# Output weight's fourth tile staged in the other weight pool, and eight woven products moved ahead of the first carry's key norm

## The chip, the cores and the metric

The kernel runs on one core of one Trainium2 chip. Such a core has a matrix engine (PE, with a weight-load path that the profile calls PEld), a vector engine (DVE), an activation engine (ACT), a general engine (POOL) and a queue engine (SP) that issues most transfers. All work on a common on-chip memory, and PE's results land in PSUM banks from which DVE and ACT read them. The metric is the device time of one execution in microseconds (us); less is better.

## The reference

One layer of a network is applied to 128 context tokens and 512 latent tokens of width 1024 (640 columns together). The layer has two branches, a recurrence over time with eight heads of 64 in two directions and an attention; their outputs are gated, summed and multiplied by the output weight `w_out`, and a feed-forward block follows:

```python
merged = (jax.nn.sigmoid(gate_rw) * (o_rw @ p["w_o_rwkv"])
          + jax.nn.sigmoid(gate_na) * (o_na @ p["w_o_na"]))
x = x + g1 * (merged @ p["w_out"])
h2 = _rmsnorm(x, p["norm2_g"]) * (1.0 + sc2) + sh2
x = x + g2 * ((jax.nn.silu(h2 @ p["ffn_w1"]) * (h2 @ p["ffn_w3"])) @ p["ffn_w2"])
```

In the recurrence the keys are normalised per head (the "key norm"): `kk = kk * lax.rsqrt(jnp.sum(kk * kk, axis=-1, keepdims=True) + L2_EPS)`. Everything is float32.

## The kernel before, in words

**Products.** A float32 factor is split into a high part `hi` and a rest `lo`, and a product is made of three matmuls, hi·hi, hi·lo and lo·hi. A weight tile of 128 x 1024 is loaded by SP into a staging buffer `wst` (`wdma`, line 166), and `wcast` (line 187) makes `whi` and `wlo` from it. On one path ACT makes `whi` (line 194) and DVE the rest (line 197). On the other path (`eng is pool`) ACT first writes the negative high part into `wlo` (line 192), POOL then issues a transfer that adds `wst` onto it (line 193), and ACT makes `whi` as well. A tile's products can start once its `whi` is there, and those with `wlo` once the transfer has landed.

**Weight pools.** `weights(stack, n, m)` opens a pool with n staging buffers and m pairs of `whi` and `wlo`; the buffers of a pool are used in turn, so a new tile waits until the tile that had the buffer is through. The first pool (index 0) has two of each and lives to the end. A second pool with two of each is opened at line 1731 for the first half of the output weight, and closed again at line 1738; at line 1761 a third pool with one staging buffer and two pairs takes its place, and its memory, like that of the residual `x2` and the gate rows `G` (lines 1741 and 1750), lies where the second pool and its neighbours were. From line 1762 on `rot` holds pool 0 and the third pool, and `wdma` takes them alternately.

**Output weight.** `w_out` has eight tiles: 0 to 3 give the first 512 output columns, 4 to 7 the other 512. `tok_gen` (line 289) goes through a list of tiles: for each it calls `wload` and yields one matmul at a time over five token blocks (30 per tile). Tile 0 (`c0`) is loaded at line 1700 into pool 0, tiles 1, 2 and 3 into the second pool; with two buffers there, tile 3 takes those of tile 1. Tile 4 is the next to use pool 0, where it follows the last merge tile (`b3`); tile 5 goes to the third pool, 6 to pool 0 after `c0`, 7 to the third. The matmuls of tile 0 are partly interleaved with the last merge (`last_gen`). Between the halves DVE adds the gated first half to the residual (`add_gated`, lines 1757 and 1758), which reads `G` and `x2` and frees the PSUM banks that the second half then takes. The feed-forward's first two tiles (`W` in the table `n2`) follow in the same staging buffers.

**The weave.** In the recurrence stage (four groups `ct` of two heads, each with `main`, `inv`, `carry`, `out`) the small matmuls of a dependent chain are interleaved with big independent ones, "products", drawn from the stream `fill` (line 803): projections, gates and merges of 48 or 36 matmuls each. The table `PRM["plan"]` says for each step of each stage how many products go ahead (first number), and then by how much of the side work goes on (line 1617). In the carry the side work is the preparation of the next group, `prep` (line 1635): ACT squares the keys (line 662), five column blocks of two matmuls each sum them (line 666), then the low-rank projections follow (lines 647 and 649), and later a transposition (line 681). `beside` (line 522) draws on it within a budget and runs due deferred steps first. All products left over are drawn by `need` at line 1701.

**Order.** In these stages the order of PE (and inside most blocks also of ACT, DVE and POOL) is that of the program. SP's order is not: the framework's scheduler places its transfers by its own timeline. SP works strictly in its order, so a transfer that waits for its buffer holds up those behind it. In the block of lines 1733 to 1737 only PE and DVE are in program order, so the scheduler places ACT's and POOL's casts there too.

Of the kernel before, what the change touches and what calls it, by code (L numbers as in the profile page):

```python
# [27 lines left out]
    order=("l0 l1 k0 r0 v0 l2 g0 g1 g2 k1 g3 r1 g4 g5 v1 g6 g7 k2 r2 g8 g9 v2 g10 g11 k3 r3 g12 g13 v3 g15 g14 a0 a1 a2 "  # L28
     "a3 b0 b1 b2 b3"),
# [2 lines left out]
        ("0.0.0 2.0.0 2.0.1 4.0.0 2.0.1 2.0.1 4.0.1 4.0.1 4.0.1 2.0.0 4.0.0 2.0.0 2.0.0 10.0.0 2.0.0 "  # L32
         "2.0.0 2.0.0 10.0.0 2.0.0 2.0.0 2.0.0 2.0.0 2.0.0 2.0.0 2.0.0 2.0.0 2.0.0 2.0.0 2.0.0 2.0.0 "
         "5.0.0 24.0.0 20.0.0 10.0.0 8.0.0 8.0.0 0.0.0"),
        ("10.0 1.0 7.1 5.2 0.0 7.1 7.2 0.0 7.1 7.2 0.0 8.1 12.2 0.0 7.1 7.2 0.0 7.1 7.2 0.0 6.1 6.2 "
         "0.0 8.1 7.2 6.0"),
        "22.0 2.0 2.0 2.0",
        ("6.0.0 0.0.0 2.0.1 4.0.0 1.0.0 2.1.1 2.1.1 2.1.1 2.1.1 1.1.1 10.0.0 3.1.0 2.0.0 2.0.0 2.0.0 "
# [72 lines left out]
def V(ap, dims, off=0):  # L111

    return bass.AP(ap.tensor, ap.offset + off, [list(ap.ap[0])] + [list(d) for d in dims])
# [3 lines left out]
def body(ctx: ExitStack, tc: tile.TileContext, xs, xp, cols, consts, w_ada, b_row, w_rw, w_qkv,  # L117
# [3 lines left out]
    pe, act, dve, pool, sp = nc.tensor, nc.scalar, nc.vector, nc.gpsimd, nc.sync  # L121
# [13 lines left out]
    wpool, rot = [], []  # L135
# [8 lines left out]
    def nm(s):  # L144
        cn[0] += 1
        return f"{s}_{cn[0]}"
# [16 lines left out]
        return K[64 * h:64 * h + 64, KO["ident"] + 64 * h:KO["ident"] + 64 * h + 64]  # L163


    def wdma(src, home=None):
        if len(rot) > 1 and home is None:
            rot.append(rot.pop(0))
        pl, nst, nhl = (rot if home is None else wpool)[-1 if home is None else home] if rot else wpool[-1]
        st = pl.tile([P, 1024], F32, tag="wst", bufs=nst, name=nm("wst"))  # L170
        n = src.shape[1]
        if len(src.shape) == 3:
            sp.dma_start(V(st[:, :], [[src.shape[2], n], [1, src.shape[2]]]), src)
            n *= src.shape[2]
        else:
            sp.dma_start(st[:, :n], src)
        return st, n, pl, nhl

    pend, off, hold, gtag = [], [0], [False], ["fl"]
# [1 line left out]
    def later(fn, cost=(0.5, 0), more=0):  # L181
        if off[0]:
            pend.append([off[0] + more, cost, fn])
        else:
            fn()

    def wcast(w, eng=None):
        st, n, pl, nhl = w
        hi = pl.tile([P, 1024], F32R, tag="whi", bufs=nhl, name=nm("whi"))
        lo = pl.tile([P, 1024], F32R, tag="wlo", bufs=nhl, name=nm("wlo"))  # L190
        if eng is pool:
            act.activation(lo[:, :n], st[:, :n], AF.Copy, scale=-1.0)  # L192
            pool.dma_start(lo[:, :n].bitcast(F32), st[:, :n], accum_op=ALU.add)  # L193
        act.copy(hi[:, :n], st[:, :n])  # L194
        if eng is not pool:
            def low(a, b):
                dve.tensor_tensor(out=lo[:, a:b], in0=st[:, a:b], in1=hi[:, a:b].bitcast(F32), op=ALU.subtract)  # L197

            if len(gtag) > 1:
                low(0, 512)  # L200
                later(lambda: low(512, n), (0, 0), -off[0] + 5)
            else:
                low(0, n)
        return hi, lo

    def wload(src, eng=None):
        return wcast(wdma(src), eng)
# [22 lines left out]
    def drain(g):  # L230
        for _ in g:
            pass
# [56 lines left out]
    def tok_gen(pss, pp, lhs_hl, chunks, kts, toks, tag="acc", bufs=5, tail=1, keep=None, eng=None, late=()):  # L289


        pss.update((i, pp.tile([P, 512], F32, tag="tp" if i == 5 else tag, bufs=3 if i == 5 else bufs,
                               name=nm("acc"))) for i in toks)
        lhs = lhs_hl if callable(lhs_hl) else lambda p_, kt, ts_: lhs_hl[p_][:, kt, ts_]
        last = len(kts) - 1
        ws, n0 = [] if keep is None else keep, len(chunks) - tail
        for ci, src in enumerate(chunks):
            ws.append(src if isinstance(src, (tuple, list)) else wload(src, eng))
            ks = [2 * ci + k for k in range(2)]

            if ci >= n0:
                order = [(ki, i) for i in toks for ki in range(2 * n0, last + 1)] if ci == len(chunks) - 1 else ()
            else:
                order = [(ki, i) for tk in (toks[:4], toks[4:]) for ki in ks for i in tk]
            ns = ((0, 1), (2,)) if ci in late else ((0, 1, 2),)
            for n, ki, i in ((n, *p_) for g in ns for p_ in order for n in g):
                kt = kts[ki]
                hi, lo = ws[ki // 2]
                ts_ = slice(min(i, 4) * 128, min(i, 4) * 128 + 128)
                a, b = (256 * (i - 4), 256 * (i - 3)) if i > 3 and 5 in toks else (0, 512)  # L310
                cs_ = slice(ki % 2 * 512 + a, ki % 2 * 512 + b)
                for x, w in (((0, hi), (1, hi), (0, lo))[n],):
                    pe.matmul(pss[i][:, a:b], lhs(x, kt, ts_), w[:, cs_], start=ki == 0 and n == 0,  # L313
                              stop=ki == last and n == 2)
                    yield
# [124 lines left out]
    def blkch(b):  # L440
        return [w_qkv[b * 4 + q] for q in range(4)]
# [80 lines left out]
    def beside(gen, budget):  # L522

        a = d = 0
        while a < budget[0] and d < budget[1]:
            if pend and pend[0][0] <= 0:
                _, c, fn = pend.pop(0)
                fn()
            else:
                c = next(gen, None)  # L530
                if c is None:
                    return
            a, d = a + c[0], d + c[1]
# [308 lines left out]
    with s1:  # L842
# [25 lines left out]
        with s1a:  # L868
            for b, dst, gcol in ((0, qT, dcol(dqg)), (1, kT, col("kg"))):
                pss = tok_block(pp, (hh, hl), blkch(b), list(range(8)), range(5)) if b else psq  # L870
# [9 lines left out]
                for i in range(5):  # L880
# [21 lines left out]
                    for f in range(4):  # L902
                        src = pst[:, f * 128:(f + 1) * 128]
                        if i < 4:
                            out = V(dst[f], [[1, 2], [8, 64]], 2 * i)
                            src = V(src, [[64, 2], [1, 64]])
# [8 lines left out]
            pss = tok_block(pp, (hh, hl), blkch(2), list(range(8)), range(5))  # L915
# [20 lines left out]
        with ExitStack() as s1b:  # L936
# [128 lines left out]
            with tc.manual_schedule(engines=FIRST):  # L1065
                for k, step in enumerate(PRM["na"].split()):
                    a, p, b, q, n, s_ = (int(x) for x in (step + ".0").split(".")[:6])
# [31 lines left out]
    with ExitStack() as s3:  # L1099
# [542 lines left out]
        with tc.manual_schedule(engines=FIRST):  # L1642
# [4 lines left out]
            for ct in range(4):  # L1647
# [8 lines left out]
                late = [lambda: st_load(0, 0, act), lambda: st_load(0, 1, act)] if ct == 0 else []  # L1656
# [43 lines left out]
            c0 = wload(w_out[0], pool)  # L1700
# [25 lines left out]
    def w_out_gen(pss, ws, toks, **kw):  # L1726
        return tok_gen(pss, pp, (mh, ml), ws, list(range(8)), toks, **kw)

    pss = {}
    trp = open_pool(hs, "trp")  # L1730
    weights(hs, 2, 2)
    w0 = w_out_gen(pss, [c0] + [w_out[q] for q in range(1, 4)], range(5), eng=pool, late=(0, 1, 2))
    with tc.manual_schedule(engines=MANUAL | {mybir.EngineType.DVE}):
        for h, _ in enumerate(last_gen()):
            for _ in range(PRM["lw"][h]):
                next(w0)
        drain(w0)
    hs.close()
    nstack.close()
    xpool = open_pool(ctx, "xpool")  # L1740
# [127 lines left out]

    with tc.manual_schedule(engines=FIRST):
        w1s = []  # L1870
        beside(w_out_gen(pss, [wload(w_out[4], pool)] + [w_out[4 + q] for q in range(1, 4)], (0, 1, 2), tail=2, keep=w1s))
        beside(w_out_gen(pss, w1s, (3, 4), tail=2))
    hstack.close()

# [363 lines left out]
    with tc.manual_schedule(engines=FIRST):  # L2238
# [8 lines left out]
        for part, fs in enumerate(fts):  # L2247
# [3 lines left out]
            for j, ft in enumerate(todo):  # L2251
# [13 lines left out]
                n = len(todo)  # L2265
# [18 lines left out]
            for n in range(2):  # L2284
                pss = {}
# [117 lines left out]
```

## Time and profile before

| | us |
|---|---|
| time, median of 3 runs | 1138.34 |
| lowest and highest run | 1136.46, 1139.86 |
| the profiled execution's own time | 1138.35 |
| its span, first to last instruction | 1136.2 |
| PE busy in the span | 1100.7 |
| DVE, ACT, POOL busy | 811.7, 571.5, 244.4 |
| mean granted PE clock | 0.995 |

A view of the timeline gives the start of a row of like instructions in us from the span's start, their time together, engine, line, operation, output and inputs, their count, and in brackets how long the engine stood idle just before and which engine's work ended that. The view of waits sums such idle times by who waited for whom: us in total, times, longest. The view of stretches gives, for each stretch of time, its length, busy us and instruction count of each engine, then the granted PE clock (1.00 is full speed), the busy share of the transfer engines and their rate. A row "SPq" is a transfer's place in SP's queue; its time spans from the first to the last issue of the row, waits between them included.

### The profile page before, as it was taken

How to read it: one execution, taken by the hardware profiler on the slowest of the kernel's cores; microseconds unless marked ns; L12 is line 12 of the kernel's file. 1: busy time of each engine (PE TensorE's matmuls, PEld its weight loads, DVE VectorE, ACT ScalarE, POOL GpSimd, SP SyncE). 2: the span in 40 equal slices, each digit the busy share in tenths (PEclk: the TensorE clock that was granted, in tenths of full speed). 3: DMA queues.
4: the chain of work that ended last, by engine and by line, in shares of the span. 5: the costliest groups of instructions: out<-in, count | busy, mean ns of one | idle time of the engine just before them, and what ended most of it. 6: DMA issues, size and time to landing. Idle time of an engine off the chain costs nothing. (4 is left out here: it accounts for less than half of the span.)

```text
span 1136.2 us, 27125 instructions
## 1 busy us (share of the span) xinstructions
PE 1100.7 (97%) x11118; PEld 973.2 (86%) x11118; DVE 811.7 (71%) x1709; ACT 571.5 (50%) x1106; POOL 244.4 (22%) x318
## 2 busy tenths in 40 slices
PE   6999999999999999999999989999999999999998
PEld 4688878799888988888898768998999989989987
DVE  4565465769558947945787826899788888889854
ACT  4444566664565565567443424564453543444430
POOL 1163244320101112110100421151212112131100
PEclk9999999999899999999999999999999999999999
DMA  9862687654423443343734773476567567675622
GB/s 342 271 116 87 203 276 241 200 153 130 105 65 92 115 128 94 93 124 93 267 107 129 237 220 114 146 184 173 144 170 183 144 162 177 164 176 140 159 86 93
DMA packets 72995, 179.05 MB, mean 158 GB/s; under 512 B 8708, under 2 KB 23684, under 8 KB 72872
## 3 DMA queue, kind: packets, MB, share of 16 engines
q1 hardware_dynamic: 58488, 140.86, 37.8%
q0 software_dynamic: 12368, 33.56, 16.2%
q10 hardware_dynamic: 2016, 2.90, 0.8%
q8 instruction: 87, 1.43, 0.5%
q14 instruction: 36, 0.29, 0.1%
HBM read 137.81 MB, written 16.94 MB: 136 GB/s over the span
## 5 line engine op out<-in xcount | busy, mean ns | idle before, releaser
L1932 PE MATMUL f<-t,whi 128*128 128x320 f32 x640 | 141.8, 309 | 1.1 <-ACT whi L1977 0.8
L1932 PE MATMUL f<-b,whi 128*128 128x320 f32 x608 | 135.0, 310 | 0.4 <-DVE b L214 0.4
L225 PE MATMUL fl<-h,whi 128*128 128x320 f32 x672 | 122.5, 321 | 0.7 <-ACT U L542 0.7
L1932 PEld LDWEIGHTS f<-t,whi 128*128 128x128 f32 x640 | 106.9, 188 | 1.9 <-ACT whi L1977 1.3
L225 PEld LDWEIGHTS fl<-h,whi 128*128 128x128 f32 x672 | 101.2, 188 | 6.1 <-ACT U L542 0.9
L1932 PEld LDWEIGHTS f<-b,whi 128*128 128x128 f32 x608 | 101.8, 188 | 1.2 <-issue 0.6
L1932 PE MATMUL f<-t,wlo 128*128 128x320 f32 x320 | 99.0, 309 | 0.2 <-DVE wlo L1980 0.2
L1932 PE MATMUL f<-b,wlo 128*128 128x320 f32 x304 | 94.0, 309 | 0.1
L194 ACT CAST whi<-wst 128x1024 fp32r<-128x1024 f32 (+1 forms) x67 | 69.0, 1031 | 49.5 <-PE acc L313 34.3
L313 PE MATMUL acc<-whi,h 128*128 128x512 f32 x240 | 77.8, 398 | 1.3 <-DVE h L438 1.1
L1977 ACT CAST whi<-ws 128x1024 fp32r<-128x1024 f32 x40 | 42.1, 1052 | 68.6 <-PE f L1932 40.1
L197 DVE TENSOR_TENSOR wlo<-wst,whi 128x1024 fp32r<-128x1024 f32 (+2 forms) x47 | 48.0, 1032 | 26.2 <-ACT whi L194 25.5
L193 POOL DMA_DIRECT2D wlo<-wst x28 | 24.9, 890 | 186.8 <-ACT wlo L192 171.1
L225 PE MATMUL fl<-h,wlo 128*128 128x320 f32 x336 | 62.3, 317 | 0.0
L1932 PEld LDWEIGHTS f<-t,wlo 128*128 128x128 f32 x320 | 60.1, 188 | 0.5 <-DVE wlo L1980 0.5
L1932 PEld LDWEIGHTS f<-b,wlo 128*128 128x128 f32 x304 | 57.1, 188 | 0.4 <-DVE wlo L1980 0.4
L1991 POOL TENSOR_TENSOR ws<-wst 128x512 f32<-128x512 f32 x20 | 30.6, 1530 | 122.2 <-DVE wlo L1980 81.7
L1980 DVE TENSOR_TENSOR wlo<-ws,whi 128x1024 fp32r<-128x1024 f32 x40 | 53.6, 1340 | 4.1 <-ACT whi L1977 4.1
L1475 DVE TENSOR_TENSOR ZV<-w,Dt 64x128 f32<-64x128 f32 x64 | 18.5, 289 | 53.1 <-PE w L1463 51.9
L313 PEld LDWEIGHTS acc<-whi,h 128*128 128x128 f32 x240 | 44.6, 188 | 13.3 <-issue 2.0
L225 PEld LDWEIGHTS fl<-h,wlo 128*128 128x128 f32 x336 | 51.2, 188 | 1.8
L984 POOL TENSOR_TENSOR L<-L,m 128x384 f32<-128x384 f32 (+1 forms) x40 | 32.1, 824 | 92.5 <-DVE m L983 68.6
(381 smaller groups left out, 2827.2 us busy)
## 6 DMA issues: line engine op xcount, KB each, us to landing
wst<-in_w_dram SPq DMA_DIRECT2D x58, 512.0 KB
wst<-in_w_rw_dram SPq DMA_DIRECT2D x31, 512.0 KB
wlo<-wst POOLq DMA_DIRECT2D x28, 512.0 KB, 4.5
wa<-in_w_ada_dram SPq DMA_DIRECT2D x22, 512.0 KB
f<-in_w_ada_dram SPq DMA_DIRECT2D x18, 512.0 KB
t<-in_w_dram SPq DMA_DIRECT2D x16, 512.0 KB
wst<-in_w_qkv_dram SPq DMA_DIRECT2D x12, 512.0 KB
o<-o_d SPq DMA_DIRECT2D x14, 320.0 KB
```

The lines of the kernel that those rows point to most:

```text
L193: pool.dma_start(lo[:, :n].bitcast(F32), st[:, :n], accum_op=ALU.add)
L194: act.copy(hi[:, :n], st[:, :n])
L197: dve.tensor_tensor(out=lo[:, a:b], in0=st[:, a:b], in1=hi[:, a:b].bitcast(F32), op=ALU.subtract)
L225: pe.matmul(ps[:, :t1 - t0], w[:, a:a + 128], x[:, k0 + kt, t0:t1], start=n == 0, stop=n == 3 * nk - 1)
L313: pe.matmul(pss[i][:, a:b], lhs(x, kt, ts_), w[:, cs_], start=ki == 0 and n == 0, stop=ki == last and n == 2)
L984: pool.tensor_tensor(out=L, in0=L, in1=V(m[:, :], [[0, w]], 3), op=ALU.mult)
L1475: dve.tensor_tensor(out=V(ZV[own, l + 1, h, :], [[128 * dl, 2], [1, 64]]), in0=V(pn[own, :], [[64, 2], [1, 64]], 64 * g), in1=V(Dt[own, 0, ...
L1932: pe.matmul(ps[:, :H2], w_[:, c_], x_[:, kt, :], start=first and kt + n == 0, stop=last and kt == 3 and n == 2, skip_group_check=more)
L1977: act.copy(r[0][:, :width], src())
L1980: dve.tensor_tensor(out=r[1][:, :width], in0=src(), in1=r[0][:, :width].bitcast(F32), op=ALU.subtract)
L1991: eng_x(PRM["se"][i - 1]).tensor_tensor(out=o_, in0=x, in1=y, op=op)
```

## The change

Three edits:

1. In the plan of the first carry (`ct` = 0) the fourth entry, at the end of the first step, is 13.2 where it was 5.2: thirteen products instead of five are drawn there before the side work with the key norm's matmuls goes on. All other entries stay, so each later point of the plan has drawn eight products more, until the last `need` draws eight fewer.
2. Tile 3 of the output weight is handed to `tok_gen` as a function, called when its turn comes, which loads it into pool 0 (`wdma(w_out[3], 0)`) and casts it on the POOL path as before. In pool 0 it takes the buffers of `b3`; tile 4 then takes those of `c0`, tile 6 those of tile 3, and the feed-forward's first tile those of tile 4. `wdma` gets its pool from `wpool[home]` also while `rot` is empty.
3. Loads made by `wdma` with a plain source after tile 4, within the second half's first block (tiles 5, 6, 7 and the feed-forward's first two), get an order without a wait: they stand behind tile 3's load in SP's queue.

```diff
-        ("10.0 1.0 7.1 5.2 0.0 7.1 7.2 0.0 7.1 7.2 0.0 8.1 12.2 0.0 7.1 7.2 0.0 7.1 7.2 0.0 6.1 6.2 "
+        ("10.0 1.0 7.1 13.2 0.0 7.1 7.2 0.0 7.1 7.2 0.0 8.1 12.2 0.0 7.1 7.2 0.0 7.1 7.2 0.0 6.1 6.2 "
...
+    sent, behind = [], [None]
+
     def wdma(src, home=None):
         if len(rot) > 1 and home is None:
             rot.append(rot.pop(0))
-        pl, nst, nhl = (rot if home is None else wpool)[-1 if home is None else home] if rot else wpool[-1]
+        pl, nst, nhl = wpool[home] if home is not None else (rot or wpool)[-1]
...
-            sp.dma_start(st[:, :n], src)
+            sent.append(sp.dma_start(st[:, :n], src))
+            if behind[0]:
+                tc.add_manual_dep(sent[-1].ins, behind[0].ins.name, mybir.DependencyInfo(
+                    mybir.DependencyClass.NoSync, mybir.DependencyReason.DATA), reason="order")
...
-            ws.append(src if isinstance(src, (tuple, list)) else wload(src, eng))
+            ws.append(src if isinstance(src, (tuple, list)) else src() if callable(src) else wload(src, eng))
...
-    w0 = w_out_gen(pss, [c0] + [w_out[q] for q in range(1, 4)], range(5), eng=pool, late=(0, 1, 2))
+    w0 = w_out_gen(pss, [c0, w_out[1], w_out[2], lambda: wcast(wdma(w_out[3], 0), pool)], range(5), eng=pool, late=(0, 1, 2))
...
         drain(w0)
+    third = sent[-1]
...
-        beside(w_out_gen(pss, [wload(w_out[4], pool)] + [w_out[4 + q] for q in range(1, 4)], (0, 1, 2), tail=2, keep=w1s))
+        w4 = wload(w_out[4], pool)
+        behind[0] = third
+        beside(w_out_gen(pss, [w4] + [w_out[4 + q] for q in range(1, 4)], (0, 1, 2), tail=2, keep=w1s))
+        behind[0] = None
         beside(w_out_gen(pss, w1s, (3, 4), tail=2))
```

## The prediction

> **What bounds the kernel now.** I read the page first, then PE's waits, then the granted clock in stretches of 1 us over the whole span, then the timelines of the two places that the change touches.
>
> ```profile
> span 1136.2 us, 27125 instructions
> ...
> PE 1100.7 (97%) x11118; PEld 973.2 (86%) x11118; DVE 811.7 (71%) x1709; ACT 571.5 (50%) x1106; POOL 244.4 (22%) x318
> ```
>
> PE is busy 97% of the span and no other engine comes near. What can be won without taking work away is PE's idle time, and time in which PE runs slowly. PE's own waits, longest in total first:
>
> ```profile
> PE psa L263 <- DMA wa<-in_w_ada_dram: 6.8, 2, 6.5
> PE acc L313 <- DMA wlo<-wst: 3.8, 1, 3.8
> ...
> PE fl L225 <- DVE mx L1585: 1.8, 3, 0.7
> ...
> PE w L666 <- ACT pre L662: 1.2, 1, 1.2
> ```
>
> The first belongs to the start and is not touched. The second is the output weight's fourth tile (tile 3), whose `wlo` transfer is late; the last is the key norm's first matmul in the first carry. Together they are 5.0 us of idle time. The stretches show that they cost more:
>
> ```profile
> 300.00:301.00 1.00, 0.01 (x1) 0.01 (x1) 0.15 (x1) 1.00 (x3) 0.61 (x2) 1.00 0.33 66
> 301.00:302.00 1.00, 1.00 (x7) 1.00 (x7) 0.00 (x0) 0.39 (x1) 0.93 (x2) 0.75 1.09 217
> 302.00:308.00 6.00, 6.00 (x87) 5.55 (x88) 0.17 (x1) 1.95 (x4) 2.17 (x5) 0.50 0.66 177
> 308.00:309.00 1.00, 1.00 (x14) 0.89 (x11) 0.00 (x0) 0.47 (x3) 0.00 (x0) 0.83 0.21 47
> ...
> 673.00:674.00 1.00, 1.00 (x5) 0.80 (x4) 0.00 (x0) 0.00 (x0) 0.00 (x0) 0.78 0.29 98
> 674.00:677.00 3.00, 3.00 (x9) 2.33 (x8) 1.69 (x3) 0.00 (x0) 0.00 (x0) 0.50 0.91 307
> ```
>
> The third number from the right is the granted clock. Behind each of the two waits it is 0.50: from about 301.5 (0.75 in the stretch 301 to 302) to 308.3, and from about 673.6 to 677. Apart from the last 2 us of the span these are the only stretches below full clock, so both slow stretches stand with the two waits that the change goes for. I price each wait with its slow stretch.
>
> **The carry: 8 products ahead of the key norm.** PE around it in the first carry, then the same place in the second carry, then ACT in the first:
>
> ```profile
> 298.80 1.00 PE L225 MATMUL fl<-h,wlo 128*128 128x320 f32 x5
> 300.99 1.87 PE L666 MATMUL w<-K,pre 128*128 128x2 f32 x10 [1.19 <-ACT pre L662]
> ...
> 311.66 0.71 PE L681 MATMUL w<-K,pre 128*128 128x128 f32 x5
> ```
>
> ```profile
> 396.90 1.29 PE L225 MATMUL fl<-h,whi 128*128 128x320 f32 x7
> 398.03 1.17 PE L666 MATMUL w<-K,pre 128*128 128x2 f32 x10
> ...
> 405.54 0.71 PE L681 MATMUL w<-K,pre 128*128 128x128 f32 x5
> ```
>
> ```profile
> 298.93 1.03 ACT L194 CAST whi<-wst 128x1024 fp32r<-128x1024 f32 x1
> 299.86 0.61 ACT L625 CAST uh<-upw 128x512 fp32r<-128x512 f32 x1
> 300.38 1.01 ACT L662 ACTIVATE pre<-kt__626,C 128x320 f32<-128x320 f32 x2
> ```
>
> PE's five products end at 299.80 and ACT, behind two casts, has the first half of the squares only at about 300.95. Eight products at the second carry's pace (398.03 - 396.90 over 7, 0.161 each) last 1.29, so they cover the 1.19. They are no extra work: the products left for the last `need` are eight fewer. They are the second half of a gate whose first half the five end, with the same weight and a free bank, so they bring no wait.
>
> The slow stretch is priced by the second carry, where between the key norm and the transposition lie the same matmuls (14 products, 8 of lines 647 and 649, the same steps of the chain) at full clock: 405.54 - 398.03 = 7.51, against 311.66 - 300.99 = 10.67 here. That is 3.16. Sum of this part: 1.19 + 3.16 = 4.35. Bounds: 1.19 if the clock drops all the same; 0 if the eight products, drawn early, only make PE wait at the end of the stream, where it waits 1.8 for DVE anyhow (the row of line 1585 above) - that would take back 1.2. A side effect is that the gate's deferred tanh is due inside this step and takes budget from one low-rank projection, which goes two entries later, where the budget that the tanh had is free. I count it at nothing.
>
> [...]
>
> **The output weight: tile 3 in pool 0.** PE in its first half:
>
> ```profile
> 654.11 4.70 PE L313 MATMUL acc<-whi,m 128*128 128x512 f32 x20
> 658.64 2.43 PE L313 MATMUL acc<-wlo,m 128*128 128x512 f32 x10
> ...
> 667.71 0.61 PE L313 MATMUL acc<-whi,m 128*128 128x512 f32 x2
> 668.25 0.65 PE L1781 MATMUL pc<-K,arow 2*128 2x2 f32 x8
> 672.68 0.50 PE L313 MATMUL acc<-wlo,m 128*128 128x512 f32 x1 [3.77 <-DMA wlo<-wst]
> ...
> 680.57 0.39 PE L313 MATMUL acc<-wlo,m 128*128 128x512 f32 x1
> ```
>
> At full clock a matmul takes (658.64 - 654.11) / 20 = 0.2265. From 672.68 to 680.57 there are 28 starts, so 27 steps: 6.12 at that pace, 7.89 measured, 1.77 lost to the slow clock. With the wait this is 3.77 + 1.77 = 5.54.
>
> Why the transfer is late, and what the new place does (ACT, POOL, SP):
>
> ```profile
> 637.41 1.06 ACT L192 ACTIVATE wlo<-wst 128x1024 fp32r<-128x1024 f32 x1 [0.72 <-PE fl L225]
> ...
> 661.15 1.05 ACT L194 CAST whi<-wst 128x1024 fp32r<-128x1024 f32 x1 [4.18 <-PE acc L313]
> ```
>
> ```profile
> 663.46 0.88 POOL L193 DMA_DIRECT2D wlo<-wst  x1 [2.68 <-ACT wlo L192]
> ```
>
> ```profile
> 623.66 0.43 SPq L176 DMA_DIRECT2D wst<-in_w_out_dram  x1
> ...
> 640.57 0.33 SPq L176 DMA_DIRECT2D wst<-in_w_out_dram  x1
> ...
> 657.37 0.33 SPq L176 DMA_DIRECT2D wst<-in_w_out_dram  x1
> ...
> 658.53 1.78 SPq L1746 DMA_DIRECT2D x<-in_xs_dram  x4
> ...
> 661.19 11.83 SPq L1752 DMA_DIRECT2D G<-adr  x2
> 673.11 10.37 SPq L176 DMA_DIRECT2D wst<-in_w_out_dram  x2
> ```
>
> Tile 3 is loaded at 657.37 and cast at 661.15, when tile 1's products have ended. Its transfer leaves at 663.46, among the residual and `G`, and PE resumes 9.2 later. Meanwhile tile 4, needed only after tile 3, was loaded at 623.66 and cast at 637.41 in `b3`'s buffers. The change swaps them: tile 3 gets that place and is ready some 20 us before 667.71. Tile 4 goes where tile 6 was loaded (640.57, when `c0`'s transfer was through with its buffer) and is cast once tile 0's products have ended, just before 654.11. Even if it left as late as 663.46 it would be there at 672.7, while its first product comes, with the wait gone, at about 668.9 + 28 x 0.2265 = 675.2. Tile 6 takes tile 3's buffers, free by then, with 36 products of tiles 4 and 5 (8.2 us) over its cast. All this is hidden, and costs nothing while that cover holds.
>
> Late next would be DVE's `add_gated`, which frees the banks for tile 4 and needs the residual and `G`:
>
> ```profile
> 674.07 0.69 DVE L1757 SCALAR_TENSOR_TENSOR tt<-acc,G 128x512 f32<-128x512 f32 x1 [19.27 <-PE acc L313]
> ```
>
> Here it waited for PE, so the first `G` had landed by 674.07. The second `G` stood in SP's queue until 672.7 because its memory was read by tile 3's transfer; in the change tile 1's is the last there, so it and tile 5 leave some 10 us earlier. With `G` at 672.8 at the latest, the third bank is free five DVE steps of 0.72 later, at 676.4, and is wanted at 675.2 + 6 x 0.2265 = 676.6. So I take 0, with 1.5 as the upper bound. The new order behind tile 3 adds no wait: tile 3's load leaves long before those put behind it, nor does SP have anything new to wait for.
>
> **The sum.** 4.35 + 5.54 = 9.89 off the profiled execution's 1138.35 (span 1136.2 and 2.15 around it), which is the median of the runs, 1138.34, to 0.01. What follows is PE-bound (its later waits in that view are below 0.8 each), so the gain carries to the end: 1128.5. Bounds of the forecast itself: 1.2 back at the stream's end and 1.5 at `add_gated` give 1131.2; up to 2 of the waits at line 1585 gone with eight products fewer there give 1126.5.
>
> **The rivals.**
>
> *The slow clock in the carry stays.* The small matmuls of the chain and the two-column ones of line 666 may be what lets the clock fall, and they stay. For it: the 3 us before 301.5 hold light work beside the wait. [...] Against it: the second carry has the same light work at full clock. Then the gain is 1.19 + 5.54: 1131.6.
>
> *A new wait in the output weight.* `G`, tile 4 or tile 5 land late because the residual, `G` and tile 5 now leave together, and PE waits 2 to 4, with a slow stretch of 1.77 behind it. For it: transfers are at a share near 1 there, and tile 3's took 9.2. Against it: tile 3's own load and transfer have left this stretch. Gain 4.35 + 5.54 - 4 to 6: 1132 to 1134.
>
> *The change doesn't do what it says.* The scheduler leaves tile 3's load where it was, and SP's new order binds others to it. Then only the carry gains: 1134.0. Against it: tile 4, later in the program, was placed at 623.66 as soon as its buffer was free.
>
> *Slower.* The feed-forward's first tile now waits for tile 4's transfer. If SP's order keeps it ahead of the residual's loads, these wait with it. Loads and `G` took from 658.53 to at most 672.7, 14.2. If they start at T, the second half's first matmul comes at T + 14.9 in place of 675.2. With T = 672.7 (tile 4 cast as late as tile 3 was) PE waits 12.4 and 1.77 more: 14.2 - 9.9 = 4.3 slower, 1142.6. It decides from T = 668.4 on. Against it: SP's rows follow readiness before.
>
> **How the numbers follow.** About 0.3% (3.4 us) can be told from no change. The forecast has 0.62, the slow clock that stays 0.12, the new wait 0.12, the change without effect on tile 3 0.06, slower 0.05, and some other reshuffle of SP's order with little net change 0.03. The range 1126.3 to 1132.5 holds the forecast with its bounds, the first rival and a little of the second. Faster by over 0.3% (below 1134.9) are the first three and most of the fourth: 0.85; within 0.3% 0.10; slower 0.05.
>
> **What would show it.** Right: no wait at lines 666 and 313 in PE's waits; clock 1.00 near 300 and 670; key norm to transposition in about 7.5; the fourth tile's 30 matmuls in one row of 6.8; the second `G` leaving right behind the first. Wrong: a new PE wait for `G`, `x` or `wst` after the first half, or a clock of 0.50 behind a key norm that no longer waits, or tile 3's load still near 657.

## The result and the profile after

| | before | after |
|---|---|---|
| time, median of 12 runs each, us | 1137.19 | 1141.39 |
| lowest and highest | 1134.31, 1142.49 | 1138.80, 1142.82 |
| profiled execution, its span | 1138.35, 1136.2 | 1140.94, 1139.1 |

The ratio after to before is 1.0031, with a 95% interval of 1.0017 to 1.0045: the change makes the kernel some 3.5 us slower (4.2 between the medians), where 9.9 us faster was forecast. Of the eleven runs of one version below (e2), two took 2096 and 3628 us for a reason that isn't known; its figures are those of the other nine. First the top of the page and PE's waits of the kernel after (lines of the helpers are 2 to 9 further down than before: 225 is now 230, 313 is 318, 666 is 671, 681 is 686, 1450 is 1455).

```profile
span 1139.1 us, 27130 instructions
PE 1099.5 (97%) x11118; PEld 970.9 (85%) x11118; DVE 814.6 (72%) x1709; ACT 572.1 (50%) x1106; POOL 244.5 (21%) x318
```

```profile
PE w L1455 <- ACT x L1429: 4.8, 6, 2.0
PE w L1406 <- ACT ZV L1461: 4.0, 1, 4.0
...
PE w L1149 <- ACT pre L1144: 2.8, 2, 2.0
...
PE fl L594 <- DMA wlo<-wst: 1.3, 1, 1.3
```

PE's work is the same in count and time. The two waits that the change went for are gone from the list. In their place stand waits for ACT, at lines that neither the change nor the prediction had looked at: 4.8, 4.0 and 2.8 where the kernel before had 1.3, 0 and 0.6 (in its view of waits line 1450 has 1.3, 1144 has 0.6, and 1401 isn't listed). PE's timeline after, at the two places the change aims at:

```profile
301.05 1.34 PE L230 MATMUL fl<-h,whi 128*128 128x320 f32 x8
302.40 0.84 PE L671 MATMUL w<-K,pre 128*128 128x2 f32 x6
...
310.02 0.71 PE L686 MATMUL w<-K,pre 128*128 128x128 f32 x5
...
676.53 0.62 PE L318 MATMUL acc<-whi,m 128*128 128x512 f32 x2
...
683.42 1.15 PE L1787 MATMUL pc<-K,arow 2*128 2x2 f32 x16
```

Every sign that the prediction named for its success is there. The key norm follows its thirteen products without a gap and reaches the transposition in 310.02 - 302.40 = 7.62 (7.5 was forecast); tile 3's 30 products run in 683.42 - 676.53 = 6.89 (6.8). The granted clock (third number from the right) says the same at 302 to 308, and then shows where it went:

```profile
302.00:308.00 6.00, 5.98 (x107) 5.39 (x106) 0.17 (x1) 3.38 (x10) 3.54 (x6) 1.00 0.91 234
...
319.00:322.00 3.00, 3.00 (x13) 3.00 (x13) 0.00 (x0) 0.68 (x3) 0.00 (x0) 0.50 0.73 143
...
438.00:442.00 4.00, 3.95 (x21) 3.84 (x22) 3.93 (x5) 1.74 (x4) 1.56 (x4) 0.57 0.65 129
...
469.00:473.00 4.00, 4.00 (x19) 4.00 (x18) 4.00 (x17) 1.35 (x2) 0.00 (x0) 0.60 0.63 120
```

The two slow stretches of before are gone, and three new ones stand behind new waits. To see where time is won and lost, this table sets the start of the same matmul in each profiled execution against its start before (us; the rows are the first instances in PE's timeline of the lines named, in lines of before):

| matmul | before | after | eight alone (e2) | given back (e3) | one load moved (e8) |
|---|---|---|---|---|---|
| first carry, transposition, 681 | 311.66 | -1.64 | -0.18 | -4.10 | -1.09 |
| second group, 1191 | 344.65 | +1.68 | +1.59 | -4.11 | -1.07 |
| third group, 1191 | 437.25 | +8.14 | +8.18 | -4.10 | -1.04 |
| fourth group, 1191 | 535.87 | +9.48 | +9.72 | -4.25 | -1.19 |
| merge, 1717 | 637.21 | +8.62 | +9.28 | -4.36 | +1.15 |
| feed-forward, 1932 | 711.78 | +3.29 | +3.97 | -8.18 | -4.36 |

A column's level holds what happened ahead of the first carry too, which scatters: in e6 below the program is that of before up to the key norm, and that starts at 303.38 in place of 300.99. Only differences between the rows of a column are read here.

After: between the transposition and the fourth group the kernel loses 9.48 + 1.64 = 11.1, and PE's new waits there for ACT, one by one in the timeline, are 2.02, 0.83, 0.84, 1.00, 4.04 and 2.00, together 10.7; one of 1.26 for a weight's transfer comes at 543.78. Some waits of before are gone, so PE's idle time in that stretch (its length less PE's busy time) grows by less, from 6.3 to 15.3, and some 2 of the 11.1 are left to the slow stretches. From the merge to the feed-forward it wins 8.62 - 3.29 = 5.33, about the 5.54 of the prediction.

**What PE waits for.** ACT around the longest new wait, after (with the place of the second wait of 2.0 behind it) and then before, and PE's row after:

```profile
435.25 0.71 ACT L558 ACTIVATE vp<-U,D 128x512 f32<-128x512 f32 x1
435.86 1.04 ACT L197 ACTIVATE wlo<-wst 128x1024 fp32r<-128x1024 f32 x1
436.80 1.03 ACT L199 CAST whi<-wst 128x1024 fp32r<-128x1024 f32 x1
437.74 0.54 ACT L1461 COPY ZV<-w 64x128 f32<-64x128 f32 x2
...
466.65 1.03 ACT L199 CAST whi<-wst 128x1024 fp32r<-128x1024 f32 x1
467.58 0.72 ACT L1144 COPY pre<-r 128x640 f32<-128x640 f32 x1
```

```profile
430.05 1.02 ACT L553 ACTIVATE vp<-U,D 128x128 f32<-128x128 f32 x2
430.97 0.53 ACT L1456 COPY ZV<-w 64x128 f32<-64x128 f32 x2
431.52 1.06 ACT L192 ACTIVATE wlo<-wst 128x1024 fp32r<-128x1024 f32 x1
432.48 1.04 ACT L194 CAST whi<-wst 128x1024 fp32r<-128x1024 f32 x1
```

```profile
438.05 0.98 PE L1406 MATMUL w<-TG,ZV 128*64 128x64 f32 x8 [4.04 <-ACT ZV L1461]
```

Before, the copy of `ZV`, on which the chain hangs, stood ahead of the two casts of a weight. After, the casts stand ahead of the copy, and so do two others ahead of the copy at 467.58, for which PE waits 2.00. Nobody moved them by hand. The stream `fill` counts products: a cast falls due when so many products of its weight's predecessor have been drawn (line 821 of before), and the tanh and other deferred steps likewise. With eight products drawn early, all of them come up eight products earlier in the program, and ACT takes them in the order of the program: in the trace the copy starts at 437.74, within 0.1 of the end of the cast before it (436.80 + 1.03).

**Two corrections.** The text above says that the eight products are given back at the last `need` (line 1701). They are given back in the third carry already, where `need("r3", "v3")` draws what is left of those projections; so the stream runs eight products ahead from the first carry to the third. And the feed-forward's first two tiles are loaded in the second `beside` block, where no order is set; only tiles 5, 6 and 7 stand behind tile 3.

### The profile page after: what moved, and what is told of

Same layout as the page of the kernel before. It is cut to its first block, busy times and chain, and to the rows that moved or that the text cites. A ratio compares the mean times of both kernels' runs of the same rounds, so it can differ in the third digit from the quotient of the medians.

```text
span 1139.1 us, 27130 instructions
## 1 busy us (share of the span) xinstructions
PE 1099.5 (97%) x11118; PEld 970.9 (85%) x11118; DVE 814.6 (72%) x1709; ACT 572.1 (50%) x1106; POOL 244.5 (21%) x318
## 5 line engine op out<-in xcount | busy, mean ns | idle before, releaser
L230 PE MATMUL fl<-h,wlo 128*128 128x320 f32 x336 | 67.3, 331 | 0.3 <-DMA wlo<-wst 0.3
L230 PEld LDWEIGHTS fl<-h,wlo 128*128 128x128 f32 x336 | 53.9, 196 | 3.3 <-DMA wlo<-wst 0.5
```

Source lines behind the costliest of these rows:

```text
L230: pe.matmul(ps[:, :t1 - t0], w[:, a:a + 128], x[:, k0 + kt, t0:t1], start=n == 0, stop=n == 3 * nk - 1)
```

## The experiments

Theory A, from the trace above: the output weight's part works; the eight products move deferred steps of ACT ahead of copies that PE waits for. Rival B: the output weight's part is what costs, through SP's order. All versions were timed in five rounds against the kernel before on the same chip. The last column is the mean over a version's runs of (1 - granted clock) x span, that is what the half clock took at most. It is contained in the times, and it scatters: in the kernel before it is 6.0 to 7.6 from round to round, so a difference of 1 to 2 us between two versions may be this alone.

| version | ratio to before (95%) | profiled span | to half clock |
|---|---|---|---|
| before (112 runs) | | 1136.2 | 6.7 |
| the change (12 runs) | 1.0031 (1.0017 to 1.0045) | 1139.1 | 6.7 |
| e1 output weight alone | 0.9978 (0.9965 to 0.9991) | 1131.2 | 5.8 |
| e2 eight products alone | 1.0045 (1.0027 to 1.0062) | 1139.6 | 8.8 |
| e3 change, given back at once | 0.9948 (0.9928 to 0.9968) | 1127.6 | 3.0 |
| e4 change, all deferred steps later | 1.0020 (1.0006 to 1.0034) | 1138.5 | 7.5 |
| e5 as e3, `G` first | 0.9924 (0.9898 to 0.9950) | 1127.9 | 1.1 |
| e6 as e1, `G` first | 0.9949 (0.9928 to 0.9969) | 1129.8 | 4.3 |
| e7 eight products, given back at once, alone | 0.9992 (0.9974 to 1.0010) | 1133.9 | 6.4 |
| e8 one load moved in SP's queue | 0.9953 (0.9936 to 0.9970) | 1131.2 | 4.2 |
| e9 change, two casts later | 1.0029 (1.0014 to 1.0045) | 1140.9 | 6.2 |
| e10 e7 and e8 together | 0.9946 (0.9925 to 0.9967) | 1133.4 | 2.9 |
| e11 change, given back at the carry's end | 0.9970 (0.9957 to 0.9984) | 1131.9 | 5.1 |
| e12 as e9, `G` first | 0.9997 (0.9985 to 1.0010) | 1135.1 | 5.4 |
| e13 change, `G` first | 1.0038 (1.0021 to 1.0055) | 1139.0 | 8.7 |

### The two parts, each alone (e1, e2)

e1 is the changed kernel with the old plan, e2 the old kernel with the new one:

```diff
-        ("10.0 1.0 7.1 13.2 0.0 7.1 7.2 ...
+        ("10.0 1.0 7.1 5.2 0.0 7.1 7.2 ...
```

> The output weight's part alone (tile 3 in the first pool, later loads behind it); the plan of the first carry as before. Theory A (phase: the eight products, never given back until the third carry, bring casts and other deferred ACT work in front of the copies that the carry's chain waits for, and this alone made the change slower): tile 3's wait of 3.8 and its slow stretch of 1.7 go, nothing else changes, 5.4 us faster, ratio about 0.995. Rival B (the new order of loads and casts costs elsewhere what it wins): same or slower, 0.999 to 1.003.

> The eight products alone; the output weight as before. Theory A: 7 to 10 us slower, ratio 1.006 to 1.009, with the same new waits of PE for ACT in carries one to three as the changed kernel, and tile 3's wait as before. Rival B: about 4 us faster, 0.996, as the key norm's wait and its slow stretch are gone.

e1 is 0.9978, e2 1.0045. The eight products alone are at least as slow as the whole change (the intervals overlap), so rival B falls and theory A has the slowdown in the right part; its sizes, 0.995 and 1.006 to 1.009, were both missed. e1 wins 2.5 us in place of 5.5, and the table of starts has a surprise: e2, in which the output weight is untouched, wins there just what the change does (9.28 - 3.97 = 5.31), and tile 3's wait isn't in its profile. Both points were followed up (e8, e6).

### When the eight are given back (e3, e11)

e3 draws four fewer at each of the two next steps; e11 only at the end of the first carry:

```diff
-        ("10.0 1.0 7.1 13.2 0.0 7.1 7.2 0.0 7.1 7.2 0.0 8.1 12.2 ...
+        ("10.0 1.0 7.1 13.2 0.0 5.1 5.2 0.0 5.1 5.2 0.0 8.1 12.2 ...
```

```diff
-         "0.0 8.1 7.2 6.0"),
+         "0.0 4.1 3.2 6.0"),
```

> Both parts, but the eight products are given back in the next four plan entries (5.1 5.2 0.0 5.1 5.2 for 7.1 7.2 0.0 7.1 7.2), before the first new wait of the changed kernel; from there on every entry has drawn as many products as before the change. Theory A: the new waits are gone and both gains stay, 8 to 10 us faster, ratio about 0.992, perhaps 1 us less because four entries cover the chain with two products fewer each. Rival C (products are missed wherever they are taken away; the place where they were drawn before needed them): the four thinner entries bring waits of 2 us or more and perhaps a slow stretch, 0.995 or above.

> The changed kernel with the eight products given back at the last steps of the first carry (8.1 7.2 becomes 4.1 3.2) in place of the third carry: from the second carry on the engines' order is that of the version that gave them back at once. Theory A (each later step that runs eight products ahead has its own price, as deferred steps come up ahead of copies that PE waits for): the waits of the second and third group (1.0, 4.04, 2.0) go, the one of 2.02 in the first carry stays; 2 to 3.7 us more than the version that gave them back at once (0.9948): 0.9975 (0.9955 to 0.9995). Rival B (the loss is made in the first carry and only shows later): no better than the changed kernel, 1.002 to 1.004.

e3 gives 0.9948: with the eight back in their place within the carry, ACT's order is that of before but for one swap in the carry and those of the output weight, of the new waits only 0.77 of the first is left (at 314.62), and 9.5 us (1.0031 - 0.9948) come back. That is 5.9 us faster than before and short of the 8 to 10 expected; part of what is missing is in the output weight, as e5 shows. e11 gives 0.9970: the wait of 2.03 behind the transposition stays, those of the second and third group go. So of the 9.5 about 2.5 us (0.9970 - 0.9948) are lost in the first carry's later steps and 6.9 (1.0031 - 0.9970) in the groups behind it. Each step that runs eight ahead has its own price.

### Which steps on ACT (e4, e9, e12, e13)

e4 makes all deferred steps due eight products later while the stream is ahead, e9 only two casts, the one shown above and the next that stands ahead of a copy (line 1144). First e4's lines, then e9's:

```diff
+                lag = 8 if (13, 24) <= (i, j) and i <= 28 else 0
+                off[0] = off[0] and PRM["off"] + lag
-                if j == n // 8:
+                if j == n // 8 + lag:
...
-                if j == (n // 2 if n == 48 else n // 4) and i + 2 < len(us):
+                if j == (n // 2 if n == 48 else n // 4) + lag and i + 2 < len(us):
```

```diff
-                if j == n // 8:
+                if j == n // 8 + (8 if i in (22, 24) else 0):
```

> Both parts, the eight products stay ahead as in the change, but from there to the third carry's end the loads, casts and other deferred steps that hang on a count of products come eight products later, so that ACT's order against the chain is nearly that of before. Theory A: the new waits are gone, 8 to 10 us faster, ratio 0.991 to 0.993. Rival C: the products are as far ahead as in the change, so it is as slow as the change, about 1.003.

> The changed kernel with two of ACT's deferred weight casts (those of the stream's products 23 and 25) made due 8 products later, which puts the first behind the copy of ZV at line 1461 and the second behind the copy at line 1144, where they stood in the kernel before. Nothing else of the carry's part moves. Theory A (casts drawn forward by the eight products stand in ACT's order ahead of copies for which PE waits; that is the slowdown): the waits of 4.04 near 438 and of 2.00 near 468 go; ratio to before, 1.003 for the changed kernel, falls by 6.0 to 9.4 us, to 0.9975 (0.9945 to 0.999). Rival B (the dependent chain is simply late there, since the products that used to cover it are spent; what stands ahead on ACT doesn't matter): the waits stay, under another name of the engine awaited, and the ratio is 1.001 to 1.004.

e4 missed: at 1.0020 it is nearly as slow as the change, as rival C had it, but by other waits. The waits for ACT that it aimed at are gone, but the weights are then cast too late for products that are drawn eight earlier, and PE waits for their transfer (1.66 at 384.81) and for a bank (1.85 at 396.21). With eight products drawn early, the casts come too early for the chain or, with this lag for all of them, too late for the products.

In e9 the trace does as theory A says. The same place on ACT and PE:

```profile
436.20 0.53 ACT L1461 COPY ZV<-w 64x128 f32<-64x128 f32 x2
436.75 1.06 ACT L197 ACTIVATE wlo<-wst 128x1024 fp32r<-128x1024 f32 x1
```

```profile
436.49 0.73 PE L1406 MATMUL w<-TG,ZV 128*64 128x64 f32 x8 [2.15 <-ACT ZV L1461]
```

The wait falls from 4.04 to 2.15 and the one of 2.00 is gone; what is left is owed to the steps that stand ahead of the copy still (lines 728 and 558). From the second to the fourth group the profile loses 4.2 in place of 7.8. Not all of this is waits: PE's idle time falls from 7.8 to 5.9 between the second group and the third, but is 4.9 in place of 4.6 from there to the fourth, where other waits grew as the one of 2.00 went; the other 2.0 are the change's two slow stretches there, which e9's profile hasn't. Yet the time did not move, 1.0029 where 0.9975 was expected, so the expectation missed. In that profile the output weight takes 71.55 from merge to feed-forward in place of 69.24, with a wait of 0.64 for DVE's add and the clock at 0.66 over 684 to 689; and from the fourth group to the merge it takes 102.6 in place of 100.5, with a slow stretch at 558 to 562. e12 therefore puts `G` ahead as well (the diff is under e5, below), and e13 does that alone:

> The changed kernel with the two casts made due 8 products later, as before, and with the feed-forward's first load behind the second load of G. In the version with the two casts alone the weave had won 3.3 by its profile against the changed kernel, but the output weight had a wait of 0.64 for DVE's add and a slow stretch, and the time had not moved. Theory A (the add waits for G there, which the feed-forward's first load holds up): that wait goes, the weave keeps its 3.3, ratio to before 0.9995 (0.997 to 1.0015). Rival B (what the two casts win in the weave is lost elsewhere or isn't there in the mean): 1.002 to 1.004 again.

> The changed kernel with only the feed-forward's first load put behind the second load of G: the control for the version that also had the two casts later (0.9997), while the two casts alone gave 1.0029. Theory A (in the changed kernel the weave is so late that G lands in time anyway, its profile has no wait of 0.6 for DVE's add; the two casts win 3.3 in the weave, and G's place decides only whether that is kept): no gain here, 1.002 to 1.004. Rival B (G's place alone brings the 3.6 that the two versions differ by, and the two casts nothing): 0.9985 to 1.001.

e12 is 0.9997, e13 1.0038: `G`'s place alone wins nothing in the changed kernel, and with it the two casts win 4.7 us (1.0038 - 0.9997), 3.9 against the change itself, whose interval lies wholly above e12's. The column of the half clock differs by 3.3 (8.7 and 5.4), but 1.0 of that stands in the kernel before of the two rounds as well (7.6 and 6.6), so up to 2.2 of the 4.7 are the clock's. So with `G` out of the way, casts ahead of copies cost time, by the waits in the trace and by these runs; that is some half of the 9.5 us, and the other steps were not moved one by one. How the 4.7 divide between the waits and the clock isn't settled. Why e9 lost all of it is left open: its profile gives back 2.3 and 2.1 in the two places named above, each with a slow stretch, but it is one execution of twelve, and the 0.2 us between e9 and the change have intervals of over 3 us each.

### The output weight: who is late (e8)

Tile 6's load, and nothing else, is moved in the kernel before: behind tile 2's, where the scheduler happened to put it in e2. Loads behind tile 4 get an order behind tile 2's load, as in the change's third edit, tile 3 stays in the second pool.

```diff
+    third = sent[-2]
...
+        behind[0] = third
         beside(w_out_gen(pss, [w4] + [w_out[4 + q] for q in range(1, 4)], (0, 1, 2), tail=2, keep=w1s))
```

> The kernel before with one load moved in SP's queue: tile 6 of the output weight, which stood ahead of the four loads of the merge's rows and of tiles 1 and 2 and waited there for the transfer of tile 0, goes behind tile 2. Tile 3 stays in the second pool, the carry as it was. Theory A (the queue held by tile 6's load is what makes tile 3 late; with the eight products the scheduler happened to place it so, which is why they alone took the wait away): tile 3's wait falls from 3.8 to below 1, ratio 0.9955 (0.994 to 0.998). Rival B (tile 3's transfer is late because the transfer engines are full, or because the weave had delayed PE against them): the wait stays at 3 to 4, ratio 1.000 (0.9985 to 1.0015).

0.9953, and tile 3's wait is gone. SP's queue before (behind the load at 640.57 that the prediction quotes), in e2, and in e8:

```profile
640.96 2.89 SPq L1711 DMA_DIRECT2D tr<-trw_d  x4
643.91 0.92 SPq L176 DMA_DIRECT2D wst<-in_w_out_dram  x2
```

```profile
640.16 1.86 SPq L1711 DMA_DIRECT2D tr<-trw_d  x4
642.07 10.66 SPq L176 DMA_DIRECT2D wst<-in_w_out_dram  x3
```

```profile
632.02 1.85 SPq L1716 DMA_DIRECT2D tr<-trw_d  x4
633.92 11.34 SPq L178 DMA_DIRECT2D wst<-in_w_out_dram  x3
...
655.49 1.78 SPq L1752 DMA_DIRECT2D x<-in_xs_dram  x4
```

Before, tile 6's load waits at 640.57 for its buffer, 3.4 after the merge's first matmul (637.21), and the four rows of the merge and tiles 1 and 2 stand behind it. In e8 the rows leave at 632.02, 6.3 ahead of that matmul (638.36). The residual's loads come 17.1 behind it in place of 21.3 (655.49 - 638.36, 658.53 - 637.21). Tile 3's transfer leaves only 1.0 sooner (663.57, or 25.2 behind that matmul, in place of 26.3), but takes at most 6.4 in place of 9.2, and PE's first product with its `wlo`, at 669.93, finds it landed. That the earlier residual loads are what leaves it room is my reading; the share of each transfer isn't shown.

```profile
663.57 0.89 POOL L198 DMA_DIRECT2D wlo<-wst  x1 [3.90 <-ACT wlo L197]
```

```profile
669.35 0.65 PE L1787 MATMUL pc<-K,arow 2*128 2x2 f32 x8
669.93 0.50 PE L318 MATMUL acc<-wlo,m 128*128 128x512 f32 x1
```

The gain of 5.3 us is that of the prediction, 5.54, by an edit of one load's place. In e2 the scheduler had moved tile 6 behind tiles 1 and 2 by itself (the row of three loads at 642.07), though only the plan of the weave differs from before; the change has the merge's rows ahead of the tiles too (639.51, then four tiles from 641.41). There was no wait left for the new staging place to remove. That e8's merge starts 2.3 later against the fourth group than before (the table) is of another place: a wait of 1.72 for `o<-o_d` at 549.63, 0.49 before, and a slow stretch at 552 to 556.

### The feed-forward's first load ahead of the residual and `G` (e5, e6)

e1's output weight won only 1.45 in its profile (offsets of -3.28 and -4.73 in the table's terms). SP, DVE and PE of e1, and the stretch behind:

```profile
661.71 0.36 SPq L178 DMA_DIRECT2D wst<-in_w_dram  x1
662.17 1.80 SPq L1752 DMA_DIRECT2D x<-in_xs_dram  x4
...
664.61 1.03 SPq L1758 DMA_DIRECT2D G<-adr  x2
```

```profile
673.56 0.69 DVE L1763 SCALAR_TENSOR_TENSOR tt<-acc,G 128x512 f32<-128x512 f32 x1 [22.12 <-DMA G<-adr]
```

```profile
674.30 0.73 PE L318 MATMUL acc<-whi,m 128*128 128x512 f32 x2 [1.80 <-DVE tt L1763]
```

```profile
675.00:680.00 5.00, 4.64 (x13) 3.06 (x12) 4.93 (x8) 1.99 (x2) 0.00 (x0) 0.66 0.04 13
```

The feed-forward's first tile now follows tile 4 in its buffer, and its load, which waits for tile 4's transfer, stands ahead of the residual and `G` in SP's queue. DVE's first add waits for `G` (22.12), PE for DVE (1.80), and the clock falls (0.66 over 675 to 680). e5 and e6 put that load behind the second load of `G`:

```diff
+            gate.append(sp.dma_start(G[g], bass.AP(ad.tensor, ad.offset + g * 6144 + b * 512, [[0, P], [1, 1024]])))
...
+        behind[0] = gate[1]
         beside(w_out_gen(pss, w1s, (3, 4), tail=2))
+        behind[0] = None
```

> Both parts, the eight products given back at the two next steps, and the feed-forward's first load put behind the second load of G in SP's queue. Theory A (that load, waiting for tile 4's transfer, holds the residual and G up; what the output weight should win is partly lost there): G lands before tile 3's end, DVE's first add waits for PE and not for G, PE's 0.6 at line 318 goes, the stretch from the merge's first matmul (line 1717 of before) to the feed-forward's first (line 1932) falls from 70.8 to 69 to 70, the ratio to before from 0.9948 to about 0.9935 (0.991 to 0.996). Rival B (the residual and G wait for memory or for the transfer engines, whatever stands ahead): the same stretch of 70.8 and the same ratio, 0.9948.

> The output weight's part alone, with the feed-forward's first load put behind the second load of G. Theory A: the wait of 1.8 for DVE's add goes, and the slow stretch behind it; the stretch from the merge's first matmul to the feed-forward's first falls from 73.1 to 69 to 70, and the ratio from 0.9978 to about 0.995 (0.9925 to 0.997). Rival B: wait and ratio stay, 0.998.

e6 gives 0.9949 in place of 0.9978, e5 0.9924 in place of 0.9948, and the output weight takes 69.2 (706.00 - 636.79) and 68.8 (703.91 - 635.09) in place of e1's 73.1. In e6 the queue reads

```profile
662.29 1.01 SPq L1760 DMA_DIRECT2D G<-adr  x2
...
668.99 0.33 SPq L178 DMA_DIRECT2D wst<-in_w_dram  x1
```

and PE's view of waits has no line for DVE's add any more, though DVE still waits for `G` (16.96 until 671.26). As forecast by theory A; rival B falls. e5 is the fastest version, 1128.54 (1127.76 to 1130.81, 6 runs): 8.6 us by its ratio, of the 9.9 that the prediction had summed, are there once the two side effects are taken away. Part of this is the clock's, whose column is 1.1 in e5 against 7.0 in the kernel before of that round.

### The price of the key norm's wait, and the smallest version (e7, e10)

e7 is the kernel before with e3's plan. e10 adds e8's order to it.

> The kernel before with the carry's part alone, the eight products given back at the two next steps, so that the deferred steps stay where they were. As the prediction had it (the key norm's wait costs 1.19 and a slow stretch of 3.16, in every execution): ratio 0.996. Theory A (the slow stretch came with the wait in some executions only, so the wait is worth 1.19 and a part of 3.16): 0.9980 (0.996 to 0.9995). The late transfer of tile 3 stays, with its 3.8.

> The smallest version of both parts: the kernel before with the eight products given back at the two next steps, and tile 6's load behind tile 2's, tile 3 left in the second pool. Theory A (the two gains are of different places and add): 0.9953 of tile 6's order alone times 0.9992 of the carry's part alone, 0.9945 (0.992 to 0.997), no wait above 1 between 300 and 700. Rival B (the staging in the first pool is worth something of its own): this stays behind the version with tile 3 in the first pool and G first, 0.9924, by over 2 us.

e7: 0.9992, that is 0.9 us won, with an interval from 3.0 won to 1.1 lost. The wait is gone in it and the clock full behind it; tile 3's wait is there, 3.11 at 670.00. The forecast of 4.35 for this part is out of the interval. Why is seen in e1, in which the wait is still there; its PE row and the stretch behind it:

```profile
300.67 1.28 PE L671 MATMUL w<-K,pre 128*128 128x2 f32 x10 [1.20 <-ACT pre L667]
```

```profile
302.00:308.00 6.00, 6.00 (x117) 5.41 (x117) 0.82 (x4) 4.14 (x12) 2.10 (x4) 1.00 0.70 200
```

The same wait, 1.20 in place of 1.19, and the clock stays full. In e6 and e8 too (1.21 each) no slow stretch follows (the clock is 1.00 over 303 to 310 in e8), though both have one of 3.4 us some 10 us ahead of the key norm, at 289 to 293, where the profile before has none. The slow stretch of the profile before was one execution's; the wait doesn't bring it each time. e10 is 0.9946 as theory A has it, with no wait above 1 between 300 and 540 in its profile, but one of 2.18 for `o<-o_d` at 551.46, the place where e8 waits 1.72; its cause is open. Behind e5 it is 2.5 us, with intervals of 5 to 6 us; whether the first pool is worth something of its own, as rival B has it, stays open.

## Why the prediction was wrong

**The eight products.** The step that failed is in the carry's part: that they are no extra work and "bring no wait", with the deferred tanh as the one side effect, counted at nothing. It looked at PE's own order and at one deferred step within the same carry. All entries of the plan behind the fourth were kept, so not one step but every deferred step of three carries came up eight products early. The runs price that at 9.5 us (the change against e3), more than the two gains that the change keeps, which are 5.9 together in e3. ACT's casts ahead of copies are the part of it that was tested by itself (e12 against e13). The fault could have been seen in the trace of before: ACT's rows at 430.97 and 431.52 show a copy of the chain and a cast back to back, with only the number of drawn products to keep their order.

**The slow stretch in the carry.** 3.16 was taken as belonging to the wait. With the wait left in place it is absent in three profiles (e1, e6, e8). The whole part measures 0.9 alone, and 0.8, 2.8 and 3.4 on top of versions of the output weight's (e10 against e8, e5 against e6, e3 against e1), against 4.35. The rival in which the slow clock stays for another reason had 1.19, near the mean of these four, 2.0. As a mechanism it didn't come true: none of the eleven profiles with the eight products ahead has a slow stretch behind the key norm, and of the four with the wait (before, e1, e6, e8) one has.

**The output weight.** 5.54 was right in size: 5.8 in e6, 5.3 in e8. The reading of its cause was half right. Tile 3's transfer did run among the residual and `G`, and it does so in e8 without a wait. What made it late was that tile 6's load, which the prediction quotes at 640.57 as waiting for `c0`'s transfer, held the queue, so that all of this came later against PE; what stood behind that load was not asked. Within the full change the part wins nothing: e2 has the same 5.31 without it.

**`add_gated` at 0, upper bound 1.5.** In the change it held, since `G` landed by 682.69, 0.7 ahead of the end of tile 3's products. In e1 the wait is 1.80, then 0.36, and a slow stretch behind it. The mechanism is the one of the rival "slower", in small: the feed-forward's first load does stand ahead of the residual and waits for tile 4's transfer. Its price was too hard: in the time of before, these loads start at 665.5 in e1 (662.17 + 3.28), which by its formula makes PE wait about 5, and the two waits are 2.2 together. It costs 3.3 (e1 against e6).

**Rivals.** The one that ended on the slower side had another mechanism than the one that made the kernel slower, and none of them had the weave behind the first carry. "The change doesn't do what it says" was right in that tile 3's new place wins nothing, and for the wrong reason: tile 3 did move, and it no longer mattered. In the chances there is a slip: the first three alone are 0.86, so with most of the fourth they are more than the 0.85 that is given.

## What to carry to other kernels

Where work is drawn from a counted stream, drawing some of it early moves everything that is due by that count: give it back at the next steps, and compare the order of each engine's instructions far behind the edit, not only the engine that the edit is on. A load that waits for its buffer at the head of an in-order queue is a suspect for every lateness behind it, and moving that one load can be worth as much as a new staging place (here 5.3 us in e8 against 5.8 in e6). A slow clock behind a wait in one profile is one execution's (here one of the four profiles with the key norm's wait has it): price the wait by itself, and take the slow stretch as a chance on top.

## What the runs showed of the hardware

But for those at the very end of the span, the slow stretches before and after are all 3.4 us of half clock or twice that: (1 - 0.57) x 4 x 2 = 3.4 at 438 to 442 above, 6.8 behind the key norm before. The same lengths are seen in e1 and e9 ((1 - 0.66) x 5 x 2 = 3.4 at 675 to 680 and at 684 to 689), in e11, e12 and e13 (3.4 at 317 to 322, 485 to 490 and 468 to 472) and in e10 (6.8 at 21 to 29). Whether a wait brings one changes from execution to execution: 2.03 at 318.72 in e13 brought none (1.00 from 319 to 330), 2.02 at 318.05 in the change did. Single waits of 0.8 (483.81 in e12, with the slow stretch from 485.7) to 4.0 us (438.05 in the change) stood ahead of slow stretches, at times. What sets the lengths, and why the same wait brings a slow stretch only at times, no run shows. The scatter of the granted clock goes with most of the spread of the times: the kernel before took 1133.6 to 1135.6 in the 11 executions with a mean clock of 0.998 and 1138.0 to 1143.3 in the 18 with 0.992. Over all 112, the column of the half clock accounts for 0.64 of the variance of the time, which rises by 0.6 us for each us in that column.

What half the clock costs depends on the place. From the first carry's transposition to the second group, in the change and then in e13, which differ only in the place of a load far behind:

```profile
310.02:346.33 36.31, 33.43 (x421) 29.31 (x418) 19.46 (x33) 23.88 (x56) 2.89 (x5) 0.95 0.29 75
```

```profile
310.69:345.45 34.76, 31.87 (x421) 27.75 (x418) 19.46 (x33) 23.77 (x56) 2.89 (x5) 1.00 0.30 78
```

PE idles 2.9 in both, and the slow stretch of the change costs 1.55, nearly the 1.7 that 3.4 us of half clock can cost. From the third to the fourth group, where DVE is busy for 4.00 of the 4.00 us of 469 to 473, the change takes 99.96, and e9 without a slow stretch and with 0.2 more idle time 99.53: there it costs about 0.7.
